# Attention of layer A: its block order written out, rounds behind the key splits, sums one per weight row

## The chip, the cores and the metric

One core of a Trainium2 chip runs the whole kernel. The metric is device time in microseconds, the median of several runs. Before the change the median of three runs is 1841.03 us (1840.54 to 1841.19).

## The reference

A decoder trunk of two layers over 512 tokens of width 2048, in float32. Layer A, to which the change belongs, is attention over selected keys: an indexer scores all keys for each query, the 128 best (min(256, 512/4)) are kept, and 16 query heads in four groups, one key/value head each, attend to them. The output is multiplied by silu of a gate path and by an output matrix.

```
proj = x @ w_in
q, k, v, gate, iq, ik, iw = jnp.split(proj, SPLITS_A, axis=-1)
...
iscore = jnp.where(causal[None], iscore, -jnp.inf)
_, idx = lax.top_k(iscore, n_sel)
...
logits = jnp.einsum('bqngd,bqknd->bqngk', qg, ksel) * (HEAD_DIM ** -0.5)
wts = jax.nn.softmax(logits, axis=-1)
o = jnp.einsum('bqngk,bqknd->bqngd', wts, vsel)
...
return (o * jax.nn.silu(gate)) @ w_o
```

Layer B, stick-breaking attention over shared keys, layer norms and a gated embedding follow; the change leaves them alone.

## The kernel before

**Arithmetic.** A float32 matrix product is made of three matmuls on high and low halves (`mm3`, L144 to L147: high by high, high by low, low by high; in the records they stand as L145, L146 and L147). `split` (L140) makes the halves: ScalarE (ACT) copies the high one, VectorE (DVE) subtracts to get the low one. All ACT and DVE work goes through a helper and so carries line L118 in the profile; one tells it apart by its tiles.

**Who sets the order.** TensorE (PE) runs in the order in which the code is written (a manual schedule). ACT, DVE, GpSimd (POOL) and SyncE are ordered by the scheduler, which sorts instructions by when it thinks they can start, except those that the code pins. Work for these engines that belongs to no product waits in a queue `bg`; `pumped_at(gen, when)` runs a product turn by turn and takes one entry off the queue at the turns that `when` lists, so that entry is issued, pinned, behind that turn. `drain()` issues what is left.

**The stages the change touches**, in time order.
- Two held gate products (the loop over `held_g`, L1116): gate columns of groups 1 and 2 by a Strassen scheme, 8 weight rows of 14 turns each, 112 turns; a turn is one `mm3` of 256 columns (tile m). The queue holds, in the first, six additions that finish the keys and values (f<-f,u); in the second, the combination of the first product's seven banks in F[3], four silus in place on F[3], and a store of F[3] to DRAM (heldg, L1130), 12 entries. The second product's own combination, into the same F[3], is queued behind and falls into the next stage. wh, wl are halves of weights, sh, sl halves of their sums.
- The q3 product (L1134): the fourth group of queries, 64 turns of 512 columns (tile q), into banks 7, 0, 3 and 4. Its queue holds what is left, the `rounds` (the last rounds of the top-k search for the fourth query block: MAX8 and MATCH_REPLACE8 on DVE, then the mask am), the restoring of halves xh, xl, the turning of keys, and the splits of V and K.
- The attention blocks (the loop over g and i, L1230): four groups g, four query blocks i. `scores(g, i)` (S) makes for each of four heads one `mm3` of 128(i+1) columns into a spare bank (4, 5, 6 in rotation); DVE adds the mask and takes the row maximum into p (p<-s,am), ACT makes the exponential and its sum (p,sm), DVE the reciprocal and the normalised p. `apply(g, i)` makes for each key block four transposes into a spare bank (T, tile pt; ACT copies ph, DVE subtracts pl) and an `mm3` with V into bank 7 (V, tile o), which needs ph for its first matmul and pl for its second; behind the last V, ACT copies o into F[g]. `fill` is the plain gate product of groups 0 and 3 (f, tile g): 128 turns in banks 1, 2, 3 and 0, four per weight row; after the 64th turn `gated(0)` makes four silus (sg<-g) and four multiplications into F[0].
- S of the next block is merged with T and V of this one by `merge`, and SHARES says how many f stand among them and how many behind. Per group there are 28 f.
- At i = 3 of groups 1 and 2 the held gates come back: three tiles sg are loaded, a fourth when the first is free, and DVE multiplies F[g] by them.

Before the attention, 12 turns of f are issued and one more behind each of the first four S.

Of the kernel before, what the change touches and what calls it, by code (L numbers as in the profile page):

```python
# [13 lines left out]
AF = mybir.ActivationFunctionType  # L14
# [4 lines left out]
T = 512  # L19
# [27 lines left out]
def run(gen):  # L47
    for _ in gen:
        pass


def steps(gen, n):
    for _ in range(n):
        next(gen, None)
# [12 lines left out]
def merge(*gens):  # L67
    gens = list(gens)
    while gens:
        for g in list(gens):  # L70
            if next(g, gens) is gens:
                gens.remove(g)
            else:
                yield
# [3 lines left out]
def trunk_kernel(  # L78
# [17 lines left out]
    pe = nc.tensor  # L96
# [4 lines left out]
    class Paced:  # L101
# [3 lines left out]
        def __init__(self, engine):  # L105
            self.engine_ = engine
# [30 lines left out]
    def bank(i, name="ps"):  # L137
        return psum.tile([128, 512], F32, name=name, tag=f"bank{i}")
# [5 lines left out]
    def mm3(out, a, b, start, stop):  # L144
        pe.matmul(out, a[0], b[0], start=start, stop=False)  # L145
        pe.matmul(out, a[0], b[1], start=False, stop=False)  # L146
        pe.matmul(out, a[1], b[0], start=False, stop=stop)  # L147
# [257 lines left out]
    bg = deque()  # L405
# [14 lines left out]
    def pumped_at(gen, when):  # L420
        for i, _ in enumerate(gen):
            if bg and i in when:
                one()
            yield
# [126 lines left out]
    def gemm_s(items, C3, M):  # L551


        rows = M[0].shape[1]
        for k in range(NK // 2):
            b11, t1 = ((XH[k][:, s], XL[k][:, s]) for s in (slice(0, H), slice(H, T)))
            if C3[k][0].shape[1] == 4:
                t1 = tuple(part[:, 3] for part in C3[k])
            b21, b22 = ((XH[k + 8][:, s], XL[k + 8][:, s]) for s in (slice(0, H), slice(H, T)))
            t2, t3, t4 = ((C3[k][0][:, i], C3[k][1][:, i]) for i in range(3))  # L560
            for j in range(rows):
                pinned[0] = True
                a11, a22, a12, s1, s2, s3, s4 = next(items)
                pinned[0] = False
                terms = ((a11, b11), (a12, b21), (s2, t2), (s3, t3), (s1, t1), (s4, b22), (a22, t4))
                for i, (a, b) in enumerate(terms):
                    first, final = (j == 0, j == 1) if rows == 2 else (i % 2 == 0, i % 2 == 1 or i == 6)
                    mm3(M[i][:, j], a, b, k == 0 and first, k == NK // 2 - 1 and final)
                    yield
# [254 lines left out]
    items = Ahead(all_items(), 2)  # L824
# [290 lines left out]
    C3A = [tuple(gated_sums[:, :, part, k] for part in range(2)) for k in range(8)]  # L1115
    for n, g in enumerate(held_g):  # L1116
        M = product_banks(1 - n)
        gemm = pumped_at(gemm_s(items, C3A, M), (6, 13, 20, 27, 34, 41, 53, 65, 77, 89, 101, 104, 107, 110))
        if n == 1:
            steps(gemm, 40)  # L1120
            for k in range(4):
                steps(gemm, 16)
                turn_keys(k)
        run(gemm)
        drain()
        if n == 1:
            items = Ahead(rest_items(), 2).prime()
        bg.extend(combine(None, M, lambda i: quarter(F[3], i), u[:, :, 0:H]))
        bg.extend(lambda j=j: act.activation(F[3][:, j], F[3][:, j], AF.Silu) for j in range(4))
        bg.append(lambda g=g: nc.gpsimd.dma_start(held_g[g], F[3]))  # L1130
# [2 lines left out]
    pkv_ = ExitStack()  # L1133
    q3 = queries(3, (7, 0, 3, 4), (*range(8, NK), *range(8)), (2, 1, 0, 3))  # L1134
    gemm = pumped_at(q3, (*range(8), *range(8, 24, 2), *(i for i in range(24, 64) if i % 3)))
    bg.extend(rounds)
    steps(gemm, 8)
    pc_.close()
    pkv = pkv_.enter_context(ss(name="pkv", bufs=1, side="right"))
# [5 lines left out]
        split(*q, F[g][:, h])  # L1145
        return q

    steps(gemm, 16)
    bg.append(turned_rows(KP, lambda g: key_rows(g, slice(0, 32))))
    for t in range(4):  # L1150
        bg.append(lambda t=t: split(*V[t], Vf[:, t]))
# [1 line left out]
    for g in range(4):  # L1153
        bg.append(lambda g=g: split(*(k.rearrange("p (t s) -> p t s", t=4) for k in K[g]), key_rows(g)))
    bg.append(lambda: nc.gpsimd.dma_start(F[1], held_q[1]))
    run(gemm)
    last_turn = bg.popleft()
    drain()
# [26 lines left out]
        if i == 3 and g < 3:  # L1185
            Q[g + 1, 3] = split_query(g + 1, 3)

    def apply(g, i):
        d = slice(g * 128, (g + 1) * 128)
        po = bank(7, "o")  # L1190
        ready = []

        def values(kb, parts):
            mm3(po, [v[:, d] for v in V[kb]], parts, kb == 0, kb == i)

        p = P[i]
        for kb in range(i + 1):
            pt = spare("pt")
            for h in range(4):
                pe.transpose(pt[:, h * 128 : (h + 1) * 128], p[:, h, kb * 128 : (kb + 1) * 128], ident)  # L1200
            parts = tuple(pb.tile([128, 512], F32R, name=f"p{x}", tag=f"p{x}", bufs=2) for x in "hl")
            split(*parts, pt)
            yield
            if ready:
                values(*ready.pop())
                yield
            ready.append((kb, parts))
        values(*ready.pop())
        act.activation(F[g][:, :, i * 128 : (i + 1) * 128], po.rearrange("p (h q) -> p h q", h=4), AF.Copy)
        yield  # L1210

    def gate_tile():
        return pb.tile([128, T], F32, name="sg", tag="sg", bufs=3)
# [11 lines left out]
            gated(g, banks)  # L1225

    fill = filling()
    steps(fill, 12)
    first = scores(0, 0)
    for _ in range(4):  # L1230
        next(first)
        steps(fill, 1)
    run(first)
    SHARES = ((6, 2, 4), (8, 2, 4), (10, 5, 4), (12, 4, 3))
    for g in range(4):
        for i in range(4):
            following = scores(g, i + 1) if i < 3 else scores(g + 1, 0) if g < 3 else iter(())
            n, amid, behind = SHARES[i]
            if g == 3 and i == 3:
                n, amid, behind = 8, 1, 6  # L1240
            if g in held_g and i == 3:
                tiles = [gate_tile() for _ in range(3)]
                for h, sg in enumerate(tiles):
                    nc.gpsimd.dma_start(sg, held_g[g][:, h])
            done = 0
            for j, _ in enumerate(merge(following, apply(g, i)), 1):
                steps(fill, amid * j // n - done)
                done = amid * j // n
            if g in held_g and i == 3:
                for h in range(4):  # L1250
                    if h == 3:
                        tiles.append(gate_tile())
                        nc.gpsimd.dma_start(tiles[3], held_g[g][:, 3])
                    dve.tensor_tensor(F[g][:, h], F[g][:, h], tiles[h], ALU.mult)
            steps(fill, behind)
    run(fill)
    pb_.close()
    pkv_.close()
# [492 lines left out]
    with tc.tile_pool(name="sp", bufs=1) as sp:  # L1751
# [14 lines left out]
        def beside(gemm, pieces):  # L1766

            for k in range(NK // 2):
                for piece in pieces.get(k, ()):
                    paced(*piece) if isinstance(piece, tuple) else paced(piece)  # L1770
                    steps(gemm, 1)
                steps(gemm, 4 - len(pieces.get(k, ())))
            run(gemm)
# [121 lines left out]
    class Sticks:  # L1895
# [101 lines left out]
        def turn(self, s, gaps):  # L1997

            late = self.diagonal(s)
            new = 1 < s < 10  # L2000
            if new:
                strictly(self.logits, s)
                if late:
                    strictly(self.low, s - 1)
                    others(3)
                strictly(self.soft, s)
                if not late:
                    strictly(self.plus, s)
                    feed(1)
            gate(gaps[0])  # L2010
            if s > 1:
                strictly(self.values, s - 2)
            gate(gaps[1])
            if s < 11:
                strictly(self.weights, s - 1)
                if new and late:
                    strictly(self.plus, s)
                strictly(self.halves, s - 1)
                if late or s == 1:
                    feed(1)  # L2020
                if s < 10:
                    strictly(self.high, s)
                    if not self.diagonal(s + 1):
                        strictly(self.low, s)
            else:
                strictly(act.preload_act_table_set, "silu_and_others")

            if self.g == 3:
                bg.extend(lambda n=n: split(*plain(n), fblock(n)) for n in {4: (0,), 7: (8,)}.get(s, ()))
            if self.g < 3:  # L2030
                bg.extend(lambda i=i: split_scaled(self.g + 1, i) for i in {7: (1,), 9: (3,), 10: (0,)}.get(s, ()))
            if not late:
                for u in {6: (3,), 9: (6,), 10: (8,), 11: (9,)}.get(s, ()):
                    strictly(self.leave, u)
                feed()
                others(({3: 1, 9: 1, 10: 1, 11: 1} if self.g else {2: 1, 3: 1, 6: 1, 7: 1, 9: 2, 10: 2, 11: 2}).get(s, 0))
            gate(gaps[2])
# [130 lines left out]
```

## Time and profile before

| what | value |
|---|---|
| median of 3 runs | 1841.03 us |
| the profiled execution: its time | 1841.41 us |
| its span | 1839.7 us |
| granted TensorE clock | 1.00 |
| attention of layer A | about 445 to 615 us |

Times in the rows are microseconds from the start of the span. A row of the timeline gives start, length, engine, line, operation, output <- inputs, and in brackets how long the engine was idle ahead of it and what released it. A row of the waits gives what waited for what: total, times, longest. Ends of matmuls are modelled, so what a wait costs is read from start to start. A row that names a releaser names the one which the profile saw last.

In the block timelines, DVE and ACT run ahead of, and behind, TensorE by a few microseconds, and their busy shares in attention (122 and 102 of 170 us) leave room.

### The profile page before, as it was taken

The numbers are of one execution on the slowest core, as the hardware profiler recorded it, in microseconds if no ns is written. First come the engines' busy times: TensorE is split into PE (matmuls) and PEld (weight loads), VectorE is DVE, ScalarE is ACT, GpSimd is POOL, SyncE is SP. The second block draws the span as 40 slices with busy tenths as digits, with TensorE's granted clock in tenths as the row PEclk, the third lists the DMA queues.
The fourth block names the chain that finished last, engine by engine and source line by source line (L and its number), as shares of the span: only waits on it lengthen the run. The fifth ranks groups of instructions, "written<-read, shape, count | busy, mean of one in ns | idle before, by whom it ended". The sixth has DMA issues, their size and how long they took to land.

```text
span 1839.7 us, 27865 instructions
## 1 busy us (share of the span) xinstructions
PE 1820.0 (99%) x10040; PEld 1587.5 (86%) x10040; DVE 1529.5 (83%) x3101; ACT 1050.0 (57%) x1936; POOL 31.1 (2%) x70
## 2 busy tenths in 40 slices
PE   9999999999999999999999999999999999999998
PEld 9888888997777799888888899998888889988898
DVE  7888989976777789976568988888877889997997
ACT  4564354455665544575346444467888854456654
POOL 0001100001000000000000000000000000000000
PEclk9999999999999999999999999999999999999999
DMA  6524574345121344333437632332222245434453
GB/s 213 162 77 133 170 238 154 104 169 161 46 86 49 92 119 121 121 119 99 141 100 234 213 104 93 106 102 80 69 69 69 65 124 145 121 120 138 121 148 122
DMA packets 123467, 226.11 MB, mean 123 GB/s; under 512 B 10432, under 2 KB 40128, under 8 KB 121664
## 3 DMA queue, kind: packets, MB, share of 16 engines
q1 hardware_dynamic: 120224, 209.65, 37.4%
q0 software_dynamic: 3104, 14.68, 2.3%
q8 instruction: 78, 1.28, 0.3%
q14 instruction: 61, 0.50, 0.1%
HBM read 205.42 MB, written 16.78 MB: 121 GB/s over the span
## 4 chain that ended last, share of the span: by engine, by line
PE 93%; DVE 4%; issue 1%; DMA 1%; ACT 1%; SPq 0%; ACTq 0%; DVEq 0%; POOLq 0%
PE m L147 11%; PE m L145 11%; PE m L146 11%; PE g L145 9%; PE g L146 9%; PE g L147 9%; PE o L146 4%; PE o L147 3%; PE o L145 3%; PE q L146 3%; PE q L147 3%; PE q L145 3%; PE iq L147 1%; PE iq L146 1%; PE iq L145 1%; PE z L1965 1%
## 5 line engine op out<-in xcount | busy, mean ns | idle before, releaser
L118 ACT ACTIVATE wh<-raw 128x512 fp32r<-128x512 f32 (+3 forms) x561 | 311.2, 555 | 410.2 <-PE g L146 131.4
L118 DVE TENSOR_TENSOR wl<-raw,wh 128x512 fp32r<-128x512 f32 (+3 forms) x560 | 333.3, 596 | 137.4 <-ACT wh L118 126.3
L145 PE MATMUL g<-xh,wh 128*128 128x512 f32 x799 | 313.0, 392 | 0.0
L147 PE MATMUL g<-xh,wl 128*128 128x512 f32 x799 | 311.2, 390 | 0.0
L146 PE MATMUL g<-xl,wh 128*128 128x512 f32 x799 | 311.2, 390 | 0.0
L147 PEld LDWEIGHTS g<-xh,wl 128*128 128x128 f32 x799 | 150.0, 188 | 31.5
L145 PEld LDWEIGHTS g<-xh,wh 128*128 128x128 f32 x799 | 150.1, 188 | 30.4 <-ACT sg L118 0.3
L146 PEld LDWEIGHTS g<-xl,wh 128*128 128x128 f32 x799 | 150.1, 188 | 30.2
L118 ACT ACTIVATE sh<-f 128x512 fp32r<-128x512 f32 x121 | 75.4, 623 | 94.7 <-DVE f L118 89.6
L147 PE MATMUL m<-xh,wl 128*128 128x256 f32 x368 | 104.4, 284 | 0.7 <-DVE wl L118 0.7
L147 PE MATMUL m<-c,sl 128*128 128x256 f32 x368 | 104.5, 284 | 0.0
L145 PE MATMUL m<-c,sh 128*128 128x256 f32 x368 | 104.3, 283 | 0.0
L145 PE MATMUL m<-xh,wh 128*128 128x256 f32 x368 | 104.3, 283 | 0.0
L146 PE MATMUL m<-xl,wh 128*128 128x256 f32 x368 | 104.1, 283 | 0.0
L146 PE MATMUL m<-c,sh 128*128 128x256 f32 x368 | 104.1, 283 | 0.0
L146 PE MATMUL q<-xl,wh 128*128 128x512 f32 x256 | 100.0, 390 | 1.5 <-DVE xl L118 1.5
L145 PE MATMUL q<-xh,wh 128*128 128x512 f32 x256 | 99.9, 390 | 0.0
L147 PE MATMUL q<-xh,wl 128*128 128x512 f32 x256 | 99.8, 390 | 0.0
L146 PE MATMUL o<-xl,wh 128*128 128x512 f32 x256 | 99.8, 390 | 0.0
L145 PE MATMUL o<-xh,wh 128*128 128x512 f32 x256 | 99.6, 389 | 0.0
L147 PE MATMUL o<-xh,wl 128*128 128x512 f32 x256 | 99.6, 389 | 0.0
L118 DVE TENSOR_TENSOR sl<-f,sh 128x512 fp32r<-128x512 f32 x121 | 83.4, 689 | 18.4 <-ACT sh L118 18.3
(446 smaller groups left out, 4737.2 us busy)
## 6 DMA issues: line engine op xcount, KB each, us to landing
raw<-w_in_a SPq DMA_DIRECT2D x95, 512.0 KB, 3.6
raw<-w_in_b SPq DMA_DIRECT2D x64, 512.0 KB, 3.7
raw<-w_ple_gate SPq DMA_DIRECT2D x44, 512.0 KB, 3.8
raw<-w_o_a SPq DMA_DIRECT2D x24, 512.0 KB, 4.6
raw<-w_o_b SPq DMA_DIRECT2D x24, 512.0 KB, 4.6
f<-w_in_a SPq DMA_DIRECT2D x16, 512.0 KB, 4.7
f<-w_kv_b SPq DMA_DIRECT2D x16, 512.0 KB, 4.5
raw<-w_kv_b SPq DMA_DIRECT2D x16, 512.0 KB, 4.3
```

Of the source, the lines that this page charges most:

```text
L118: ins = method(*args, **kw)
L145: pe.matmul(out, a[0], b[0], start=start, stop=False)
L146: pe.matmul(out, a[0], b[1], start=False, stop=False)
L147: pe.matmul(out, a[1], b[0], start=False, stop=stop)
L1965: pe.matmul(z, down if kb % 2 else tri, p, start=False, stop=n == 1, skip_group_check=True)
```

## The change

The number of matmuls and of other instructions stays. (1) The list of turns at which the two held gate products pump the queue changes from a denser one (6, 13, 20, 27, 34, 41, 53, ...) to one entry in each weight row of 14 turns (10, 24, ..., 80) and then 84, 88, 92, 96, 104, 107. (2) In the q3 product `bg.extend(rounds)` moves from ahead of the key and value splits to behind them, and two more turns (18 in place of 16) go ahead of the point where those are queued. (3) `merge` and SHARES give way to a class and a table ORDERS that writes each block's order of S, T, V and f out; before the attention stand 10 f in place of 12, and the first scores have their own order.

```diff
@@ -1115,7 +1115,7 @@
     C3A = [tuple(gated_sums[:, :, part, k] for part in range(2)) for k in range(8)]
     for n, g in enumerate(held_g):
         M = product_banks(1 - n)
-        gemm = pumped_at(gemm_s(items, C3A, M), (6, 13, 20, 27, 34, 41, 53, 65, 77, 89, 101, 104, 107, 110))
+        gemm = pumped_at(gemm_s(items, C3A, M), (*range(10, 84, 14), 84, 88, 92, 96, 104, 107))
         if n == 1:
             steps(gemm, 40)
             for k in range(4):
@@ -1133,7 +1133,6 @@
...
-    bg.extend(rounds)
...
-    steps(gemm, 16)
+    steps(gemm, 18)
     bg.append(turned_rows(KP, lambda g: key_rows(g, slice(0, 32))))
...
+    bg.extend(rounds)
     run(gemm)
...
+        def turn(self):
             pt = spare("pt")
             for h in range(4):
-                pe.transpose(pt[:, h * 128 : (h + 1) * 128], p[:, h, kb * 128 : (kb + 1) * 128], ident)
+                pe.transpose(pt[:, h * 128 : (h + 1) * 128], self.p[:, h, self.made * 128 : (self.made + 1) * 128], ident)
             parts = tuple(pb.tile([128, 512], F32R, name=f"p{x}", tag=f"p{x}", bufs=2) for x in "hl")
             split(*parts, pt)
-            yield
-            if ready:
-                values(*ready.pop())
-                yield
-            ready.append((kb, parts))
-        values(*ready.pop())
-        act.activation(F[g][:, :, i * 128 : (i + 1) * 128], po.rearrange("p (h q) -> p h q", h=4), AF.Copy)
-        yield
+            self.ready.append(parts)
+            self.made += 1
...
+        def values(self):
+            d = slice(self.g * 128, (self.g + 1) * 128)
+            kb = self.used
+            mm3(self.po, [v[:, d] for v in V[kb]], self.ready.popleft(), kb == 0, kb == self.i)
+            self.used += 1
...
     fill = filling()
-    steps(fill, 12)
+    def beside(order, following, values):
+        for c in order.replace(" ", ""):
+            if c == "f":
+                steps(fill, 1)
+            elif c == "S":
+                next(following)
+            elif c == "T":
+                values.turn()
+            else:
+                values.values()
+
+    ORDERS = (
+        "S T S f S f V S ffff",
+        "S T f S T S f V S f V fff",
+        "S T f S T f V S f T V S f V fffff",
+        "S T f S T f V S T f V S T f V ff V f",
+    )
+    steps(fill, 10)
     first = scores(0, 0)
-    for _ in range(4):
-        next(first)
-        steps(fill, 1)
+    beside("S f S f S f S fff", first, None)
     run(first)
-    SHARES = ((6, 2, 4), (8, 2, 4), (10, 5, 4), (12, 4, 3))
     for g in range(4):
         for i in range(4):
             following = scores(g, i + 1) if i < 3 else scores(g + 1, 0) if g < 3 else iter(())
-            n, amid, behind = SHARES[i]
-            if g == 3 and i == 3:
-                n, amid, behind = 8, 1, 6
+            order = ORDERS[i] if i < 3 or g < 3 else "T ff T f V T f V T f V f V"
             if g in held_g and i == 3:
                 tiles = [gate_tile() for _ in range(3)]
                 for h, sg in enumerate(tiles):
                     nc.gpsimd.dma_start(sg, held_g[g][:, h])
-            done = 0
-            for j, _ in enumerate(merge(following, apply(g, i)), 1):
-                steps(fill, amid * j // n - done)
-                done = amid * j // n
+            beside(order, following, Apply(g, i))
+            run(following)
             if g in held_g and i == 3:
                 for h in range(4):
                     if h == 3:
                         tiles.append(gate_tile())
                         nc.gpsimd.dma_start(tiles[3], held_g[g][:, 3])
                     dve.tensor_tensor(F[g][:, h], F[g][:, h], tiles[h], ALU.mult)
-            steps(fill, behind)
```

Three places in the engines' order. First, TensorE near the end of a block (g, 2), while the scores of (g, 3) are made: transposes (pt), values (o) and gate turns (g). Before:

```order
L1200 MATMUL pt<-ident,p 128x128 x4
L145 MATMUL g<-xh_84,wh 128x512
L146 MATMUL g<-xl_100,wh 128x512
L147 MATMUL g<-xh_84,wl 128x512
L145 MATMUL o<-ph,vh_4147 128x512
L146 MATMUL o<-pl,vh_4147 128x512
L147 MATMUL o<-ph,vl_4148 128x512
L145 MATMUL o<-ph,vh_4149 128x512
L146 MATMUL o<-pl,vh_4149 128x512
L147 MATMUL o<-ph,vl_4150 128x512
```

After:

```order
L1197 MATMUL pt<-ident,p 128x128 x4
L145 MATMUL o<-ph,vh_4147 128x512
L146 MATMUL o<-pl,vh_4147 128x512
L147 MATMUL o<-ph,vl_4148 128x512
L145 MATMUL s<-kh_4137,qh 128x512
L146 MATMUL s<-kl_4138,qh 128x512
L147 MATMUL s<-kh_4137,ql 128x512
L145 MATMUL g<-xh_84,wh 128x512
L146 MATMUL g<-xl_100,wh 128x512
L147 MATMUL g<-xh_84,wl 128x512
L145 MATMUL o<-ph,vh_4149 128x512
L146 MATMUL o<-pl,vh_4149 128x512
```

The last o turn uses the halves of these transposes, the o turn ahead of it those of the transposes before. Before, a g and an o turn stand between the transposes and the o turn that uses them; after, an o, an s and a g turn.

Second, ACT at the end of block (1, 2), where the gate turns reach their 64th and the silus of group 0 (sg<-g) are made. Before:

```order
L118 ACTIVATE p,sm<-p,sm 128x512
L118 ACTIVATE wh<-raw 128x512
L118 ACTIVATE p,sm<-p,sm 128x512
L118 ACTIVATE f_110<-o 128x4x128
L118 ACT_TABLE_LOAD
L118 ACTIVATE sg<-g 128x512 x3
L118 ACTIVATE wh<-raw 128x512
L118 ACTIVATE sg<-g 128x512
L118 ACTIVATE ph<-pt 128x512
L118 ACT_TABLE_LOAD
L118 ACTIVATE p,sm<-p,sm 128x128
L118 ACTIVATE ph<-pt 128x512
```

After:

```order
L118 ACTIVATE wh<-raw 128x512
L118 ACTIVATE f_110<-o 128x4x128
L118 ACT_TABLE_LOAD
L118 ACTIVATE sg<-g 128x512
L118 ACT_TABLE_LOAD
L118 ACTIVATE p,sm<-p,sm 128x512
L118 ACT_TABLE_LOAD
L118 ACTIVATE sg<-g 128x512 x2
L118 ACTIVATE wh<-raw 128x512
L118 ACTIVATE sg<-g 128x512
L118 ACTIVATE ph<-pt 128x512 x2
L118 ACT_TABLE_LOAD
```

Before, the last exponential of the 512 wide scores (p,sm) stands ahead of the copy of o and of one load of the function table with the silus behind it. After, one silu stands ahead of that exponential, with a load on each side, and a third load ahead of the other silus.

Third, ACT near the end of the second held gate product; f_112 is F[3], which the first product's silus change in place, kt the turned keys. Before:

```order
L118 ACTIVATE sh<-f_109 128x512
L118 ACTIVATE wh<-raw 128x384
L118 ACTIVATE sh<-f_109 128x512
L118 ACTIVATE f_112<-f_112 128x512
L118 ACTIVATE wh<-raw 128x384
L118 ACTIVATE sh<-f_109 128x512
L118 ACTIVATE f_110<-kt 128x4x128
L118 ACTIVATE rp<-kt 32x512
L118 ACTIVATE wh<-raw 128x384
L118 ACTIVATE sh<-f_109 128x512
L118 ACTIVATE wh<-raw 128x512
L118 ACTIVATE f_110<-kt 128x4x128
```

After:

```order
L118 ACTIVATE sh<-f_109 128x512 x2
L118 ACT_TABLE_LOAD
L118 ACTIVATE f_112<-f_112 128x512
L118 ACTIVATE wh<-raw 128x384
L118 ACTIVATE f_110<-kt 128x4x128
L118 ACTIVATE rp<-kt 32x512
L118 ACTIVATE f_112<-f_112 128x512
L118 ACTIVATE sh<-f_109 128x512
L118 ACTIVATE f_112<-f_112 128x512
L118 ACTIVATE wh<-raw 128x384
L118 ACTIVATE sh<-f_109 128x512
L118 ACTIVATE f_112<-f_112 128x512
```

Before, this silu is the last of the four, the others and their table load stand further ahead, and three pairs of kt copies follow or surround it. After, the table load and all four silus stand together, and the last one is behind the last sh.

More of the change, by code (lines that the diff above doesn't have):

```diff
@@ L1186, in scores, with __init__ @@
             Q[g + 1, 3] = split_query(g + 1, 3)
[L1188 to L1197, printed above, removed]
+    class Apply:
+        def __init__(self, g, i):
+            self.g, self.i, self.made, self.used, self.ready = g, i, 0, 0, deque()
+            self.p, self.po = P[i], bank(7, "o")
+        def turn(self):
             pt = spare("pt")
             for h in range(4):
-                pe.transpose(pt[:, h * 128 : (h + 1) * 128], p[:, h, kb * 128 : (kb + 1) * 128], ident)
+                pe.transpose(pt[:, h * 128 : (h + 1) * 128], self.p[:, h, self.made * 128 : (self.made + 1) * 128], ident)
             parts = tuple(pb.tile([128, 512], F32R, name=f"p{x}", tag=f"p{x}", bufs=2) for x in "hl")
             split(*parts, pt)
-            yield
-            if ready:
-                values(*ready.pop())
-                yield
-            ready.append((kb, parts))
-        values(*ready.pop())
-        act.activation(F[g][:, :, i * 128 : (i + 1) * 128], po.rearrange("p (h q) -> p h q", h=4), AF.Copy)
-        yield
+            self.ready.append(parts)
[5 more added lines that the diff above has]
+            self.used += 1
+            if self.used > self.i:
+                out = F[self.g][:, :, self.i * 128 : (self.i + 1) * 128]
+                act.activation(out, self.po.rearrange("p (h q) -> p h q", h=4), AF.Copy)
     def gate_tile():
```

## The prediction

> **What bounds the kernel now.** I read the page first: the span, the busy shares and the chain that ended last.
>
> ```profile
> span 1839.7 us, 27865 instructions
> PE 1820.0 (99%) x10040; PEld 1587.5 (86%) x10040; DVE 1529.5 (83%) x3101; ACT 1050.0 (57%) x1936; POOL 31.1 (2%) x70
> PE 93%; DVE 4%; issue 1%; DMA 1%; ACT 1%; SPq 0%; ACTq 0%; DVEq 0%; POOLq 0%
> ```
>
> TensorE is busy 99% and is 93% of the chain. The change leaves the instructions as they are, so all it can win is TensorE's waiting: 1839.7 − 1820.0 = 19.7 us in the whole span, and what each wait costs beside its recorded length. The next view is the waits of TensorE, for the attention of layer A (445 to 615 us), and the busy time of the engines in that stretch, with the two stretches ahead of it that the change touches.
>
> ```profile
> PE o L146 <- DVE sm L118: 3.9, 6, 1.7
> PE o L146 <- DVE pl L118: 2.5, 6, 1.2
> PE s L145 <- DVE sm L118: 1.8, 5, 0.9
> PE pt L1200 <- DVE p L118: 1.2, 1, 1.2
> PE o L145 <- ACT ph L118: 0.8, 3, 0.4
> ...
> 445.00:615.00 170.00, 159.53 (x807) 128.39 (x806) 122.43 (x415) 102.37 (x235) 6.42 (x12) 1.00 0.21 59
> ...
> 307.00:321.00 14.00, 14.00 (x111) 13.69 (x110) 13.41 (x25) 7.23 (x14) 0.00 (x0) 1.00 0.26 76
> 335.00:349.00 14.00, 14.00 (x119) 14.00 (x118) 11.59 (x26) 6.68 (x14) 0.00 (x0) 1.00 0.38 114
> ```
>
> The columns of the last three are the stretch, its length, the busy time of PE, PEld, DVE, ACT and POOL, the clock (1.00) and DMA. In attention TensorE idles 170.00 − 159.53 = 10.5 us; the five rows name 10.2 of it in 21 waits. DVE works 122 of the 170 us (72%), so it isn't the bound there on average: TensorE meets single results too early. The form of the commonest wait:
>
> ```profile
> 473.95 0.60 PE L1200 MATMUL pt<-ident,p 128*128 128x128 f32 x4
> ...
> 475.78 0.40 PE L145 MATMUL o<-ph,vh 128*128 128x512 f32 x1
> 476.67 0.50 PE L146 MATMUL o<-pl,vh 128*128 128x512 f32 x1 [0.49 <-DVE sm L118]
> 477.00 0.39 PE L147 MATMUL o<-ph,vl 128*128 128x512 f32 x1
> 477.23 0.40 PE L145 MATMUL g<-xh,wh 128*128 128x512 f32 x1
> ...
> 477.93 0.40 PE L145 MATMUL g<-xh,wh 128*128 128x512 f32 x1
> ...
> 475.93 0.68 DVE L118 TENSOR_TENSOR pl<-pt,ph 128x512 fp32r<-128x512 f32 x1
> ```
>
> Transposes start at 473.95; their low half pl runs on DVE until 476.61, and the second matmul of V, at 476.67, waits for it. The engine named (sm) was done; pl came last. The usual pitch is 477.23 − 477.00 = 0.23 (a turn of three, 477.23 to 477.93, takes 0.70), here 476.67 − 475.78 = 0.89 and then 0.33: 0.66 + 0.10 = 0.76 us for a recorded 0.49. **A wait costs its length plus 0.27.** The attention therefore loses 10.2 + 21 × 0.28 = 16.1 us.
>
> **The change, part by part.** *One: the q3 product, rounds behind.*
>
> ```profile
> 415.97 0.50 PE L146 MATMUL q<-xl,wh 128*128 128x512 f32 x1 [1.47 <-DVE xl L118]
> 409.53 0.69 DVE L118 MAX8 m<-wk 128x8 f32<-128x512 f32 x1
> 439.43 0.69 DVE L118 TENSOR_TENSOR wl<-raw,wh 128x512 fp32r<-128x512 f32 x1 [3.16 <-ACT wh L118]
> ```
>
> TensorE waits 1.47 us for a restored xl, ahead of which the top-k rounds stand on DVE. With 0.28 on top, −1.75 us. The rounds now come behind the splits of V and K, at the end of the product. There DVE idles (3.16 us ahead of 439.43 alone), which covers two passes like the 0.69 of 409.53, 1.4 us a round; their mask is needed only by the fourth score block. Uncovered, four rounds would be 5.6 us of DVE ahead of splits that the attention's start waits for; I take nothing, by that idle row.
>
> *Two: sums, one per weight row.* A weight row is 14 turns of three matmuls, 42 at 14.00 / 119 = 0.118 us (the stretch from 335): 4.9 us.
>
> ```profile
> 327.47 1.22 DVE L118 TENSOR_TENSOR f<-f,u 128x1024 f32<-128x1024 f32 x1
> 330.00 0.39 PE L147 MATMUL m<-xh,wl 128*128 128x256 f32 x1 [0.66 <-DVE wl L118]
> ```
>
> Adds of 1.22 us fall every 7 turns, two a weight row, and DVE is busy 13.41 of 14 us (307 to 321). At 330.00 a wl comes late behind the add of 327.47: 0.66 + 0.28, and two short gaps of 0.1 behind it, about 1.2 us. One add a row frees about 1.2 of every 4.9 us; DVE falls to the 11.59 of 14 of the stretch from 335, which has no wait. −1.2 us.
>
> The same list governs what runs beside the second product: the first product's silus and the store of its F[3]. There it delays: three of the four silus and the store come later, and the third order view shows the last silu behind the last sh.
>
> ```profile
> 379.97 0.62 ACT L118 ACTIVATE f<-f 128x512 f32<-128x512 f32 x1
> 385.12 0.62 ACT L118 ACTIVATE sh<-f 128x512 fp32r<-128x512 f32 x1
> 391.89 1.08 ACT L118 ACTIVATE f<-m 128x512 f32<-128x512 f32 x2
> 380.88 0.54 POOL L1130 DMA_DIRECT2D heldg<-f  x1 [129.83 <-ACT f L118]
> heldg<-f POOLq DMA_DIRECT2D x2, 1024.0 KB, 5.1
> f<-heldq POOLq DMA_DIRECT2D x3, 1024.0 KB, 6.9
> 393.71 0.39 PE L145 MATMUL q<-xh,wh 128*128 128x512 f32 x1
> ```
>
> Before, silu four ran at 379.97 and the store started at 380.88. Behind 385.12, with a table load and the later silus between, silu four ends near 387.8, so the store starts near 388.1 and, at 6.1 us (between the two medians 5.1 and 6.9), lands at 394.2. The second product's evacuations into the same F[3] (391.89) must wait for it, and with them the bank that q3's third turn takes at 393.71. The new wait: 394.2 + 0.6 − 393.7, +0.28, gives some +1.2 us; nothing if it lands in 5.1 with no evacuation behind it, 3.2 if two us later. I take +1.2.
>
> *Three: the written order of attention.* The number of f turns per group stays 28; T, f, S and V change places. What lies between a T and its own V is the point: before, in the (x,2) blocks, an f and another V (first order view), 1.4 us behind the T's start plus its 0.35; afterwards a V, an S and an f in that place, and everywhere 2.5 to 3.6 us by the pitches (f, V and S512 0.70, T 0.35 from 473.95 to 474.31) where T to end of pl needs 2.66 (473.95 to 476.61). So **the twelve o waits on pl or sm go**, and most of the ph and s waits. What remains or is new:
>
> ```profile
> 517.93 0.72 ACT L118 ACTIVATE p<-p,sm 128x512 f32<-128x512 f32 x1 [0.23 <-DVE sm L118]
> 518.56 0.19 ACT L118 ACTIVATION_READ_ACCUMULATOR p<-p,sm 128x1 f32 x1
> 518.65 0.60 ACT L118 ACTIVATE f<-o 128x512 f32<-128x512 f32 x1
> 519.27 1.28 ACT L118 ACT_TABLE_LOAD   x1
> 520.57 1.58 ACT L118 ACTIVATE sg<-g 128x512 f32<-128x512 f32 x3
> 519.06 0.49 DVE L118 TENSOR_SCALAR p<-p,sm 128x512 f32<-128x512 f32 x1
> 525.53 0.30 PE L145 MATMUL s<-kh,qh 128*128 128x128 f32 x1 [0.91 <-DVE sm L118]
> 533.45 1.90 DVE L118 TENSOR_TENSOR f<-f,sg 128x512 f32<-128x512 f32 x3 [1.46 <-ACT f L118]
> 537.99 0.69 DVE L118 TENSOR_TENSOR f<-f,sg 128x512 f32<-128x512 f32 x1 [0.61 <-DMA sg<-heldg]
> ...
> 534.43 3.53 DMA sg<-heldg
> ```
>
> (a) The gate boundary in block (1,2). Before, the last exp is done, then one load, three silus. Now (second order view) the scheduler sets one silu ahead of the last exp: load, silu, load, exp, load. From the last scores' end: f and V 1.4, evacuation (0.6, started 0.2 later) until 2.2, load 1.28, silu 0.5, load 1.28, exp 0.7 and its sum 0.2, p 0.5: 6.7 us, where f, V, five f and an S128 cover 5.1. T waits 1.6 + 0.28 = 1.9; the f turn whose bank the second silu frees waits 1.0 behind the third load; what takes the first T's bank, freed by a ph behind all silus, 1.2. Sum 4.1, less 0.3 shared: **3.8** (1.4 of it was there before, at 525.53; serial to the end it would be 6).
> (b) The held multiplications: three of 0.6 us and wl (0.69) stand on DVE ahead of pl; V waits 0.7 + 0.27 in (2,0) and (3,0): 1.9. Before, the fourth's tile (its DMA of 3.53, landed 537.96) held DVE ahead of a pl: the 1.7 of the first waits row, 1.9 in all; now that V has more turns ahead of it.
> (c) Block (3,1): p of the fourth head behind the next block's reduction, and the next p: 0.9 + 0.5 = 1.4. (d) The other small ones, three S at 0.1 and the last V at 0.15, with eight restarts at 0.11: 1.4.
> Together 8.5 us; attention gains 16.1 − 8.5 = **7.6**.
>
> [...]
>
> *Sum, against the profiled execution's 1841.41 us:* −7.6 − 1.75 − 1.2 + 1.2 = −9.35, so 1832.1. The median of the runs is 1841.03, 0.38 lower; **forecast 1831.7**.
>
> **The rivals.** *All stalls go:* 16.1 + 1.75 + 1.2 = 19.1, 1822. For it: 72% of DVE. Against: the three loads at the boundary stand in the order. *Half goes:* if the DVE queue, whose order the scheduler remakes, puts one wl (0.69) or a reduction like it ahead of the pl of one V in six of the eight S384 and S512 blocks, beyond what the longer distance covers, each costs 0.69 + 0.27, 5.8 in all: 1837.5. For it: DVE takes its queue in order, and this V at 476.67 was late by just such work. *No change:* the waits move from V to S and T, and attention stays at 170 us; only q3 and the first sum remain, less the DMA: 1839.3. Against: DVE has 47 us to spare there. It is also what results if a V, moved, still meets its pl. *Slower switches:* each load of (a) holds ACT for its own length once more before the next function starts, 3 × 1.28 = 3.8 on T, f and the bank behind: 1835.5; the 1.30 from 519.27 to 520.57 speaks against it. *Slower, the held store:* the store of F[3] starts 7 us later and meets q3's weights and the load of heldq on the DMA engines; nothing covers an evacuation that waits for it, and TensorE stands with the bank. It decides from 9.4 + 3.7 us of further waiting: landing at 394.2 + 13.1 = 407 gives 1845. The trace's 1 MB transfers of 5.1 and 6.9 us speak against 19.
>
> **How the numbers follow.** A measurement of this kernel can tell about 0.2% (3.7 us) from no change: faster is below 1837.3, slower above 1844.7. Forecast (1828 to 1836): 0.50. All stalls go: 0.16, faster. Half goes: 0.19, of which 0.12 on the faster side. Slower switches: 0.03, faster. No change: 0.06. Slower: 0.06. Faster 0.81, same 0.13, slower 0.06. The bounds of the boundary (1.4 to 6), the store (0 to 3.2) and (b) to (d) (0 to 4.7) make −6 to +4 about the forecast when not all fall alike; stretched to the half-gone case and part of the first, the range is **1825.0 to 1838.5**.
>
> **What would show it.** In the profile after: no wait of q on xl near 416 and none of m on wl near 330; a wait of q behind an f<-m evacuation near 394, on the store from L1130; in attention no o <- sm or pl longer than 0.3 outside (2,0) and (3,0); three ACT_TABLE_LOADs within 5 us at the boundary, with T, f and a bank waiting behind them; PE idle in the 170 us down from 10.5 to about 5. It is wrong if the o waits stay with other names, if waits on p or on banks exceed 9 us, or if the store lands in time or far later.

## The result, and the profile after

The changed kernel takes 1831.49 us (median of 4 runs, 1829.41 to 1832.19) beside 1841.11 before (4 runs, 1840.54 to 1843.03): a ratio of 0.9944, 95% interval 0.9927 to 0.9961, about 10 us faster. The forecast was 1831.7, its range 1825.0 to 1838.5. The profiled execution took 1831.24 us, its span 1829.5.

TensorE's waits over the whole span, as for before: who waits for whom, total us, times, longest.

```profile
PE pt L1197 <- DVE sm L118: 1.5, 2, 0.9
PE spun L167 <- DVE xl L118: 1.4, 1, 1.4
PE pt L1197 <- DVE p L118: 1.2, 1, 1.2
PE q L145 <- ACT f L118: 1.2, 1, 1.2
PE g L145 <- ACT sg L118: 0.9, 1, 0.9
PE s L145 <- DVE sm L118: 0.8, 2, 0.4
PE o L146 <- DVE xl L118: 0.3, 1, 0.3
PE iq L147 <- DVE wl L118: 0.2, 1, 0.2
```

The rows that carried the prediction are gone: no o on sm or pl (6.4 us in 12 waits), no q on xl, no m on wl. The one pt on p of before (1.2, at 451.97) is gone too. New are a q on f (the held store), a g on sg and the pt rows (the gate boundary, and 0.60 in block (3,1)). From the first gate turn of attention to the first matmul of the output product, by windows of each kernel (the first row is before, the second after; columns as in the prediction):

```profile
437.66:619.13 181.47, 171.00 (x857) 137.87 (x856) 127.72 (x424) 109.94 (x247) 6.42 (x12) 1.00 0.21 60
```
```profile
435.88:608.45 172.57, 168.07 (x857) 140.19 (x856) 126.70 (x424) 112.44 (x251) 6.46 (x12) 0.99 0.23 66
```

The stretch is 8.9 us shorter. The starts of these two windows differ by 1.78, the ends by 10.68; by the first m<-c,sh of the output product (663.48 before, 653.33 after) 0.53 is given back, since TensorE now meets the o <- xl wait of the list above. What was ahead: 0.30 near the start of the kernel, which the change doesn't touch, 1.17 in the first held product, 0.31 in q3. The sum is −0.30 − 1.17 − 0.31 − 8.90 + 0.53 = −10.15.

The boundary of the gate in the changed kernel, first ACT, then TensorE by the timeline:

```profile
511.44 1.28 ACT L118 ACT_TABLE_LOAD   x1
512.74 0.60 ACT L118 ACTIVATE sg<-g 128x512 f32<-128x512 f32 x1
513.36 1.28 ACT L118 ACT_TABLE_LOAD   x1
514.65 0.72 ACT L118 ACTIVATE p<-p,sm 128x512 f32<-128x512 f32 x1
...
515.48 1.28 ACT L118 ACT_TABLE_LOAD   x1
516.78 1.09 ACT L118 ACTIVATE sg<-g 128x512 f32<-128x512 f32 x2
```
```profile
516.24 0.33 PE L1197 MATMUL pt<-ident,p 128*128 128x128 f32 x1 [1.25 <-DVE p L118]
517.43 0.51 PE L145 MATMUL g<-xh,wh 128*128 128x512 f32 x1 [0.86 <-ACT sg L118]
...
519.57 0.74 PE L1197 MATMUL pt<-ident,p 128*128 128x128 f32 x4 [0.89 <-DVE sm L118]
519.98 0.76 PE L145 MATMUL g<-xh,wh 128*128 128x512 f32 x1
520.53 0.63 PE L146 MATMUL g<-xl,wh 128*128 128x512 f32 x1
520.96 0.63 PE L147 MATMUL g<-xh,wl 128*128 128x512 f32 x1
...
523.68 0.48 PE L145 MATMUL g<-xh,wh 128*128 128x512 f32 x1
```

Three loads follow one another on ACT, each function starting 1.29 to 1.30 us after its load does. Two of them are new: the kernel before has 19 such loads, the changed one 21. TensorE waits for the p of the delayed exponential, then for the second silu, then for a bank. The three spare banks are taken in rotation, so the transposes at 519.57 need the bank of the scores made at 514.20 (s), and DVE frees it by the row maximum at 519.22, which stands behind two multiplications by the silus and a wl:

```profile
517.41 1.29 DVE L118 TENSOR_TENSOR f<-f,sg 128x512 f32<-128x512 f32 x2 [1.22 <-ACT sg L118]
518.62 0.69 DVE L118 TENSOR_TENSOR wl<-raw,wh 128x512 fp32r<-128x512 f32 x1
519.22 0.28 DVE L118 CUSTOM_DVE_ANT_0 p<-s,am 128x128 f32<-128x128 f32 x1
```

And then something that the prediction did not have: from 520.53 a matmul starts every 0.43 us, not 0.23. The granted clock of these stretches is the third number from the end:

```profile
513.18:516.60 3.42, 2.14 (x12) 1.36 (x10) 1.34 (x3) 3.38 (x5) 0.00 (x0) 1.00 0.52 153
516.60:520.01 3.41, 1.69 (x11) 1.42 (x11) 2.60 (x6) 2.75 (x6) 1.13 (x2) 1.00 0.03 11
520.01:523.42 3.41, 3.41 (x12) 2.83 (x11) 1.88 (x8) 2.76 (x6) 0.55 (x1) 0.50 0.66 215
523.42:526.84 3.42, 3.42 (x22) 2.98 (x22) 3.07 (x13) 2.62 (x6) 0.00 (x0) 1.00 0.04 12
```

From 520.01 to 523.42 the granted clock is 0.50, behind 3.41 us in which TensorE was busy 1.69. The f, V, S and T that start at 519.98 take 3.70 us, until the next f at 523.68; by the pitches elsewhere (0.70 for f and for V, 0.28 for S from 514.20 to 514.48, 0.35 for T) they take 2.03. So some 1.7 us are lost there. Of the four runs, the three with a mean clock of 0.998 took 1831.24 to 1832.19, the one with 0.999 took 1829.41.

The held store, in the changed kernel's chain and then in ACT's timeline:

```profile
386.62 6.27 DMA heldg<-f
...
393.57 0.50 PE q L145
```
```profile
392.92 1.09 ACT L118 ACTIVATE f<-m 128x512 f32<-128x512 f32 x2 [1.35 <-DMA heldg<-f]
```

The store starts at 386.62 and takes 6.27 us; the evacuations behind it start at 392.92, and the third turn of q at 393.57, after a recorded wait of 1.16 us.

### The profile page after: what moved, and what is told of

It reads as the page before. It is cut to its first block, busy times and chain, and to the rows that moved or that the text cites. A ratio compares the mean times of both kernels' runs of the same rounds, so it can differ in the third digit from the quotient of the medians.

```text
span 1829.5 us, 27854 instructions
## 1 busy us (share of the span) xinstructions
PE 1816.4 (99%) x10040; PEld 1589.0 (87%) x10040; DVE 1528.4 (84%) x3101; ACT 1052.9 (58%) x1938; POOL 31.1 (2%) x70
## 4 chain that ended last, share of the span: by engine, by line
PE 97%; DVE 1%; DMA 1%; issue 1%; ACT 1%; SPq 0%; ACTq 0%; DVEq 0%; POOLq 0%
PE m L147 11%; PE m L145 11%; PE m L146 11%; PE g L145 10%; PE g L147 10%; PE g L146 10%; PE o L146 4%; PE o L147 4%; PE o L145 4%; PE q L145 3%; PE q L146 3%; PE q L147 3%; PE iq L147 1%; PE iq L146 1%; PE iq L145 1%; PE z L1974 1%
```

## The experiments

The table has the medians, and the mean clock of the profiled execution; each row's kernel before ran beside it on the same chip.

| run | median us | kernel before | ratio (95%) | clock |
|---|---|---|---|---|
| changed kernel | 1831.49 | 1841.11 | 0.9944 (0.9927 to 0.9961) | 0.998 |
| sums alone | 1845.34 | 1841.64 | 1.0020 (1.0011 to 1.0029) | 1.000 |
| rounds alone | 1841.08 | 1841.64 | 0.9994 (0.9985 to 1.0002) | 0.999 |
| orders alone | 1834.56 | 1841.64 | 0.9960 (0.9946 to 0.9973) | 0.998 |
| changed, store early | 1831.12 | 1841.64 | 0.9940 (0.9928 to 0.9953) | 0.998 |
| changed, silus behind exp | 1827.36 | 1841.30 | 0.9923 (0.9911 to 0.9936) | 1.000 |
| changed, both | 1825.65 | 1841.30 | 0.9914 (0.9901 to 0.9928) | 1.000 |
| changed, old (x,2) order | 1829.19 | 1841.30 | 0.9932 (0.9920 to 0.9945) | 0.999 |
| both, held products spread | 1824.25 | 1841.30 | 0.9906 (0.9891 to 0.9922) | 1.000 |

**The sums alone**, in the kernel before:

```diff
-        gemm = pumped_at(gemm_s(items, C3A, M), (6, 13, 20, 27, 34, 41, 53, 65, 77, 89, 101, 104, 107, 110))
+        gemm = pumped_at(gemm_s(items, C3A, M), (*range(10, 84, 14), 84, 88, 92, 96, 104, 107))
```

> The kernel before with the sums' turns alone (one per weight row). My theory: the wait of m on wl near 330 goes (-1.2 us), and the store of F[3] starts later, so that a turn of q waits near 394 for an evacuation (+1.4); but the wait of q on xl near 416 is set by VectorE's own queue with the rounds ahead, which a later TensorE doesn't lengthen, so it shrinks by about as much. Sum about -1.2: 1839.9. Rival, that the two waits add up: 1841.3. Rival, that the wait near 330 only moves to another weight row: 1841 to 1842.5.

None of the three held: 0.2% slower. In its trace the wait of m on wl is gone, and the store's wait is there, 1.2 us as in the changed kernel. But the wait of q on xl grew, from 1.47:

```profile
417.61 0.50 PE L146 MATMUL q<-xl,wh 128*128 128x512 f32 x1 [3.18 <-DVE xl L118]
...
415.59 0.69 DVE L118 TENSOR_TENSOR sw<-sw,Sq 128x512 f32<-128x512 f32 x1
416.19 0.69 DVE L118 TENSOR_TENSOR rp<-rp,Cq 128x512 f32<-128x512 f32 x1
416.80 0.42 DVE L118 TENSOR_SCALAR am<-am 128x512 f32<-128x512 f32 x1
417.13 0.42 DVE L118 TENSOR_TENSOR xl<-raw,xh 128x256 fp32r<-128x256 f32 x1
```

The scheduler set two more pieces of the turning of keys (sw, rp) ahead of that xl than in the kernel before, whose rows are

```profile
415.50 0.42 DVE L118 TENSOR_TENSOR xl<-raw,xh 128x256 fp32r<-128x256 f32 x1
415.83 0.69 DVE L118 TENSOR_TENSOR sw<-sw,Sq 128x512 f32<-128x512 f32 x1
416.43 0.68 DVE L118 TENSOR_TENSOR rp<-rp,Cq 128x512 f32<-128x512 f32 x1
```

So with the rounds where they were, the sums cost more at q3 than they save. The profiled execution is 1.87 us above that of before, the median 3.7. The profiled one, the fastest of its 11 runs, has a mean clock of 1.000. Five of the others have 0.998, which among the profiles here only the changed kernel, the orders alone and the early store have, all three with the clock at 0.50 for a time, and they took 1844.37 to 1847.16. So a half clock probably makes the rest, but this is read from mean clocks alone and not shown.

**The rounds alone**, in the kernel before:

```diff
-    bg.extend(rounds)
     steps(gemm, 8)
...
-    steps(gemm, 16)
+    steps(gemm, 18)
...
     bg.append(lambda: nc.gpsimd.dma_start(F[1], held_q[1]))
+    bg.extend(rounds)
     run(gemm)
```

> The kernel before with the rounds behind the key splits and the two more turns alone. My theory: the wait of q on xl near 416 goes, nothing comes in its place: -1.75 us, 1839.3. Rival, that the rounds at the end of q3 make the attention's first blocks late by VectorE: 1840 to 1842, with waits on p or sm between 440 and 460 that the kernel before doesn't have.

The wait at q goes and none comes in the first blocks: the first gate turn of attention starts at 435.88, where before it was 437.66. Yet the median gains only 0.6 us, within its interval. The 11 runs fall in two groups: five from 1839.14 to 1839.97, where the theory has 1839.3, and six from 1841.08 to 1842.21. The profiled execution is the slowest of these. In it the output product starts at 619.10, before at 619.13: attention lost it all again. The place is block (2,0), where the pl that V needs stands behind a held multiplication and its DMA, as in the kernel before. TensorE's row, and the busy time of the stretches around it:

```profile
537.75 0.50 PE L146 MATMUL o<-pl,vh 128*128 128x512 f32 x1 [1.88 <-DVE sm L118]
...
534.85:538.26 3.41, 1.53 (x7) 0.96 (x6) 2.55 (x9) 1.44 (x5) 0.55 (x1) 1.00 0.54 184
538.26:541.67 3.41, 3.41 (x12) 2.94 (x12) 2.17 (x11) 1.82 (x7) 0.00 (x0) 0.50 0.29 77
```

In the kernel before the same wait is 1.71 us, TensorE is busy 1.70 of the 3.41 us from 536.30 to 539.71, and the clock stays at 1.00. Here the wait is 1.88 us, TensorE is busy 1.53 of the 3.41 us up to 538.26, and the clock is 0.50 from there to 541.67. Why it fell here and not in the kernel before is not shown. This half clock is all by which attention differs from before, but for 0.2 us of the wait itself. So the move is worth 1.8 us at q3, and for one of the six slower runs it is shown where they lost it again. (Another 0.8 of that run went at a g turn that starts late, at 982.80, far behind the edit.)

**The orders alone**, in the kernel before (the class, ORDERS and `beside` of the change, and nothing else of it):

```diff
-            for j, _ in enumerate(merge(following, apply(g, i)), 1):
-                steps(fill, amid * j // n - done)
+            beside(order, following, Apply(g, i))
+            run(following)
```

> The kernel before with the written order of the attention blocks alone. My theory: the attention and the start of the output product gain what they gain in the changed kernel, 8.4 us by the two traces (-8.9 in attention, +0.5 at the first o0 turns), with the same three table loads and the lower clock behind them: 1832.7. Rival, that a share of the gain came from the rounds out of the attention's first blocks: less than 7.5, above 1833.5.

It is 7.1 us faster by the medians. The same boundary stands in its trace with the same three waits (1.3, 0.9 and 0.8), but its clock is at 0.50 for 6.8 us, beside 3.41 in the changed kernel, and attention gains 7.8 us there, not 8.9. No wait of the first blocks is new. By its median this is the rival's case, but not by its trace: TensorE's starts keep step with those of the changed kernel all through attention, except between 519 and 525 of that kernel's time, where the longer half clock takes 1.1 us. That is the difference between 7.8 and 8.9, and the rounds gave none of it. The profiled execution is the slowest of its five; it lost 0.9 us more near the start of the kernel (its first q product starts at 156.72, before at 155.78), which the orders don't touch.

**The changed kernel with the store early**:

```diff
-        gemm = pumped_at(gemm_s(items, C3A, M), (*range(10, 84, 14), 84, 88, 92, 96, 104, 107))
+        gemm = pumped_at(gemm_s(items, C3A, M), (6, 13, 20, 27, 34, 41, 53, 65, 77, 89, 101, 104, 107, 110) if n else (*range(10, 84, 14), 84, 88, 92, 96, 104, 107))
```

> The changed kernel, with the turns of before in the second held product alone, so that the silus and the store of F[3] come early again. My theory: the wait of q on an f<-m evacuation near 393.6 (1.2 us, 1.43 from start to start) goes, and the sums' gain in the first product stays: 1830.0. Rival, that without it a wait on xl takes its place since VectorE is no further ahead: 1831.4.

The median is near the rival's, but its mechanism isn't there: the wait of q on f is gone and none on xl came, and the first gate turn of attention starts at 434.50 and not 435.88. Yet the median is 0.4 lower, not 1.4. The clock is at 0.50 from 516.99 to 523.82 here, 6.83 us:

```profile
513.58:516.99 3.41, 1.30 (x7) 0.93 (x7) 1.60 (x4) 3.38 (x7) 0.00 (x0) 1.00 0.05 20
516.99:520.41 3.42, 2.69 (x12) 2.21 (x11) 3.06 (x10) 2.04 (x5) 1.68 (x3) 0.50 0.49 147
520.41:523.82 3.41, 3.41 (x13) 3.02 (x12) 1.41 (x9) 2.16 (x6) 0.00 (x0) 0.50 0.28 90
```

The boundary's three waits are there as well (1.3, 0.9 and 0.7, where the changed kernel has 1.2, 0.9 and 0.9), in an attention that starts 1.4 us earlier. Why the half clock lasts longer here is not shown.

**The silus behind the exponential**, in the changed kernel:

```diff
-            act.activation(p, p, AF.Exp, bias=nm, scale=HSCALE, accum_out=rs)
+            exps[0] = act.activation(p, p, AF.Exp, bias=nm, scale=HSCALE, accum_out=rs)
...
-            act.activation(sg, banks[h], AF.Silu)
+            with tc.issue_after(exps[0].ins):
+                act.activation(sg, banks[h], AF.Silu)
```

> The changed kernel, with the four silus of group 0 held behind the last exponential of block (1,2)'s scores, so that the functions switch once there and not three times. My theory: the three waits there (1.25 + 0.86 + 0.89 recorded, 3.6 us from start to start) go and one of about 1 us comes (the gate turn on bank 1 waits for its silu), and the half clock of 3.4 us that followed goes with them, as TensorE had been idle half of the 3.4 us ahead of it (about 2.1 us of pitch): 1831.5 - 3.6 + 1.1 - 2.1, about 1827, mean clock 1.000. Rival, that the lower clock has nothing to do with the waits: 1829, clock 0.998. Rival, that the silus behind the exponential hold the next transposes' copies as long as the loads did: 1831.

1827.36: the first theory. One load stands there in place of three, one wait in place of three, and the clock stays at 1.00 (mean 1.000):

```profile
514.36 0.50 PE L145 MATMUL g<-xh,wh 128*128 128x512 f32 x1 [0.55 <-ACT sg L118]
...
513.14:516.55 3.41, 2.86 (x16) 2.18 (x16) 2.21 (x6) 3.40 (x7) 0.59 (x2) 1.00 0.52 154
```

**Both**: the two edits together.

> The changed kernel with both: the silus behind the exponential, and the second held product pumped at the turns of before. My theory: the 1.4 us at 393.6 and the gain of the run before add up, 1825.5, since no half clock is left for a shift to change. Rival, that a later wait takes the 1.4 back: 1827.

1825.65, the first theory. With a mean clock of 1.000 in both profiles, the early store is worth what it should be: 1.7 us by the medians of this run and the one before it, and attention starts at 434.59 here and at 436.14 there.

**The old order in the (x,2) blocks**, in the changed kernel:

```diff
-        "S T f S T f V S f T V S f V fffff",
+        "S T f S T f S V f S T f V V fffff",
```

> The changed kernel with the order of before in the four (x,2) blocks (an f and a V between the last T and its V). It also puts the last exponential ahead of the silus by itself. My theory: the wait of 0.77 us returns in each of the four blocks (+3.1), the boundary loses 1.4 in place of 3.6, and the half clock goes (-4.3): 1830.3. Rival, that the distance between T and V isn't what counts: no o <- sm or pl waits at those four places, 1827.

1829.19: all its five runs (1828.81 to 1829.32) lie below the changed kernel's lowest, 1829.41, and it is nearer to the first theory, 1.1 us below it. The waits came back in three of the four blocks, not in (3,2):

```profile
512.04 0.50 PE L146 MATMUL o<-pl,vh 128*128 128x512 f32 x1 [0.46 <-DVE sm L118]
```

Each costs 0.63 + 0.11 from start to start, 2.2 us in all, and the distance between T and V is what brings them. But the exponential is again ahead of the silus, a gap of 0.2 us ahead of the transposes at 518.11 is all that the boundary keeps, the mean clock is 0.999 beside 0.998, and attention as a whole is 2.6 us shorter (170.02 beside 172.57). The new order of the (x,2) blocks gained 2.2 us and by the scheduler's answer to it lost more than twice that.

**Both, with the held products spread**:

```diff
-                for h in range(4):
+                def times(h, g=g, tiles=tiles):
...
-                    dve.tensor_tensor(F[g][:, h], F[g][:, h], tiles[h], ALU.mult)
+                    with tc.issue_after(pls[0].ins):
+                        dve.tensor_tensor(F[g][:, h], F[g][:, h], tiles[h], ALU.mult)
+                late.extend(lambda h=h, f=times: f(h) for h in range(4))
```

`pls[0]` is the newest pl, and every second f turn takes an entry off `late`.

> The run with both, and the held multiplications of groups 1 and 2 issued behind the first pl of the block after the one in which they become ready, not ahead of its reductions. My theory: the S and V waits of 0.96 us in (2,0) and (3,0) (blocks whose scores are 256 wide) go, -1.9 us: 1823.6. Rival, that what they displace (p, sm) becomes late by as much: 1825.5.

1824.25, 1.4 us of the 1.9, and all its runs (1823.87 to 1824.64) lie below those of the kernel it was made from (1824.91 to 1826.79). The s <- sm waits are gone from the list; what is left of attention beside the silu's 0.6 is the wait in (3,1), which is on p now:

```profile
PE pt L1198 <- DVE p L118: 0.7, 1, 0.7
```

It is the fastest kernel here, 0.9906 of before (0.9891 to 0.9922).

## Why the prediction was right, and where its sum was not

- *The wait of q on xl, −1.75.* Right: gone, and the rounds at the end of q3 cost nothing. The run of the sums alone shows the move is also what keeps the sums from costing 1.7 us there.
- *The sums, −1.2.* Right: 1.17, and no other wait in that product.
- *The held store, +1.2.* Right in its steps: the prediction had the store at 388.1 and its landing at 394.2 on before's clock; with the 1.47 us that the stage comes earlier, they are 388.1 and 394.4. The turn of q is 1.3 us late, 0.1 more at the restart.
- *The o waits on sm and pl go.* Right, all twelve; the old order in the (x,2) blocks brought three back.
- *The boundary, 3.8.* Right in its size and in the first two waits: 1.41 + 1.08 + 1.10 from start to start, 3.6 (forecast 1.9, 1.0 and 1.2). The third wait came by another way than the one named: not on the first T's bank, which a ph frees, but on the bank of the scores ahead of it, which DVE frees behind the silus' multiplications. That its price was near the forecast is luck. **Missing was the half clock behind it**, 1.7 us, which the silus behind the exponential took away together with the waits. The prediction looked at gaps one by one; here three came in 4.6 us (514.99 to 519.57), and the clock was 0.50 from 520.01 on.
- *The held multiplications, 1.9.* Right in size, 0.96 and 0.94; the step named V, and it was mostly S that waited (0.58 + 0.10, V 0.17 + 0.11). Spreading them took 1.4 of it.
- *Block (3,1), 1.4.* Measured 1.1: 0.76 + 0.22 and a restart.
- *The other small ones, 1.4.* Too large: beside these terms and the half clock about 0.5 is left of the loss after, 8.8 by the count below.
- *The start of the output product.* Costed at nothing; it gives back 0.53, an o on xl behind the last silus' multiplications.
- *Attention's loss before, 16.1.* Too small. Counted from start to start, every gap of more than 0.1 us over the usual pitch, the stretch loses 17.3 us before (42 gaps) and 8.8 after (27, the half clock among them), a gain of 8.5 of the 8.9; the rest is in smaller gaps. The term was made of recorded waits and one price for a restart, and a start that comes late without a recorded wait, like the 573.85 of an o behind its ph (0.22 late), is in no row of that list.

The forecast's profiled sum was 1832.1, the profile 1831.24. Of the 0.8 between, 0.30 is the kernel's start; attention with the output product's start gained 8.4 in place of 7.6, as what the sum had too little of before (1.2 and more) and the smaller waits after paid for the unforeseen half clock and the 0.53; and q3 gained 0.2 less. So the number is close partly because errors cancelled. The rival of slower switches, in which each load holds ACT for its own length once more, is refuted by the rows at 511.44 and 513.36: the next function starts 1.30 and 1.29 us after the load does.

## What to carry to other kernels

An order written by hand on one engine moves what the scheduler does on the others: look in their orders, not the hand-written one, for function switches and for pieces that now stand ahead of something urgent. Judge an edit by its own waits and by the granted clock behind the waits it leaves: here the rounds alone removed 1.8 us at q3, and in the profiled run the time came back where the clock was 0.50 for 3.41 us behind a wait (1.88 us) that before (1.71 us) had left the clock at 1.00. When parts of a change interact (sums and rounds here, orders and switches), run each alone before keeping or dropping any.

## What the runs showed of the hardware that I had not expected

The granted clock was 0.50 in the attention of four kernels: from 520.01 to 523.42 in the changed kernel, from 538.26 to 541.67 in the rounds alone, from 516.99 to 523.82 with the store early, and for 6.8 us in the orders alone. In the first two, the 3.41 us ahead of it had TensorE busy 1.69 and 1.53, with no single wait over 1.25 and 1.88 us. Neither little busy time nor a long wait was enough by itself: the sums alone have a stretch with less than the changed kernel's 1.69 that kept the clock:

```profile
412.96:416.37 3.41, 1.46 (x7) 0.88 (x5) 3.41 (x9) 0.47 (x1) 0.00 (x0) 1.00 0.31 76
```

It kept the clock although the wait of 3.18 us, the one that ends at 417.61, begins in it, and the 3.41 us behind it have 1.00 as well. What decides when the clock falls, and for how long, these runs don't show.
